# One step of a hybrid encoder layer: turning the running product of stick-breaking attention itself, with differences of v's rows, and loading the convolution's operands in pieces

## The chip, the cores and the metric

The kernel runs on one core of a Trainium2 chip. The metric is the device time of one execution in microseconds (us), the median over several runs. A TensorE is called PE below, a VectorE DVE, a ScalarE ACT, a GpSimd POOL and the engine that issues most transfers SP, as the profile names them.

## The reference

One layer over 1024 prompt frames and 32 sample frames (T = 1056 columns), D_MODEL 1024, 8 heads of 64:

```python
h = rmsnorm(x, g_mix)
q, k, v, cb, cc, cx, ga, gc = split(h @ w_in)
# stick breaking, strictly causal, per head
z = q @ k.T / sqrt(64);  mask = k_pos < q_pos
log_1m = where(mask, log_sigmoid(-z), 0)
tail = reverse_cumsum(log_1m) - log_1m          # keys after this one
a = where(mask, exp(log_sigmoid(z) + tail), 0)
y_attn = (a @ v) @ w_attn_out
y_conv = (cb * causal_conv3(cc * cx)) @ w_conv_out
x = x + (sigmoid(ga) * y_attn + sigmoid(gc) * y_conv) @ w_o
x = x + square(relu(rmsnorm(x, g_ffn) @ w_up)) @ w_down
x = x + sigmoid(rmsnorm(x, g_ple) @ w_ple_gate) * (p @ w_ple)
```

A last RMSNorm gives y; k, v and the last convolution rows are outputs too. In other words, with s = sigmoid(z), r = sigmoid(-z) = 1 - s and R[t,j] the product of r[t,i] over the keys i from j up to t-1, a weight is a[t,j] = s[t,j] R[t,j+1], which is also R[t,j+1] - R[t,j].

## The kernel before, in words

Everything is kept as channels by frames, and each float32 product on TensorE is three products of high and low parts (`wh`, `wl`; L642 to L644, L718 to L720, L932 to L934, L1616 to L1618), mostly with 128 rows, 128 columns of weights and 264 moving columns. By time the stages are:

- 0 to 332 us: the input projection `w_in`. Pairs of 512-column products are done with seven products of sums (the helper lines L213 to L215; results are put together on DVE in L249, L254, L259). What has to follow such a product (scaling by the norm, splitting, storing; `follow`, `values`, `conv_in`, `conv_gate`) is a generator in a list `side`, of which one piece is run after each product; `after(wait, gen)` lets `wait` pieces pass first. `conv_gate` (L554 to L562) forms the convolution's product with cb, splits it into high and low (`cvh` L558, L561) and stores it to `cvd`. `values` turns v (L509), splits it and stores it to `vd`. Tiles of 528 KB come from one pool (`blk`): a new tile takes a place whose last use, a transfer's reading included, has to be over.
- 332 to 629 us: attention. 64 steps (p, j, i): head pair p, head j, block i of 128 queries, which meets its i+1 blocks of 128 keys. The loop at the end of the stage goes through ORDER = "LSAFBFG": L weighs the step before (`weigh`: DVE scan L781 and product L782) and empties `pending`; S makes the scores (PE L759, L760; two sigmoids on ACT, L765; two causal fills on POOL, L773); A and B turn the step before that (`flip`: PE transposes of `s` L813, ACT cast to high L816, DVE low part L817); G gathers a finished pair of query blocks (`gather`: PE L834, ACT copy L843, DVE addition in `pending`); F fills with other TensorE work, a share given out by `spare(n)` and `shares()`: gate units, `last_gates`, `embed_unit` (L718 to L721) and `conv_unit` (weights cast L921, gate scaled on DVE L922, split L923, sigmoid on ACT L924, products L932). This part is scheduled in the written order. `conv_parts` (L857), called by the first embed unit, loads the eight 528 KB operands of the convolution from `cvd`. `branches_ahead`, after the last step, fetches and prepares the first weights of the next stage.
- 629 to 815 us: the two branch projections and `w_o`. Then the MLP: up with seven products, whose sums of the first set are made by `mid_sums(0, ...)` at once (L1396 to L1403) and of the others in `side`; mean squares of the norm (`mean_squares`, L1371); down to about 1465.
- 1465 to 1571: the gate of the embedding, in units u = 0 to 23. `post_c(u)` squares a finished unit on ACT (L1709) and adds it up on POOL (L1710). After the last unit comes `finish(23)`: sigmoid (L1764), loading of ACT's table with the root (L1765), product and residual on DVE (L1766, L1767), square (L1747), row sums on PE in two groups (`ps_early`, `ps_last`, L1740) added on DVE (L1749), root on ACT (L1750), reciprocal, three diagonals, a broadcast by PE (L1756), and the outputs.

Of the kernel before, what the change touches and what calls it, by code (L numbers as in the profile page):

```python
# [15 lines left out]
P = 128  # L16
# [33 lines left out]
def tile_step(  # L50
# [29 lines left out]
    keep = cpool.tile([P, 2, DEC], F32, name="keep")  # L80
    drop = cpool.tile([P, 2, DEC], F32, name="drop")
    for m_, a_, b_ in ((keep, 1.0, 0.0), (drop, 0.0, 1.0)):
        nc.gpsimd.memset(m_, a_)
        for p_ in range(4):
            r_ = m_[32 * p_ : 32 * p_ + 32, :, :]
            nc.gpsimd.affine_select(
                r_, r_, pattern=[[0, 2], [-1, DEC]], compare_op=ALU.is_gt, fill=b_, base=0, channel_multiplier=1
            )
# [357 lines left out]
    for p_ in range(4):  # L446
        nc.gpsimd.memset(vsT[p_], 0.0)

# [52 lines left out]
    def values(p, m):  # L501
# [3 lines left out]
        tm = blk(f"vt{p}", F32, [P, 8, P])  # L505
        for q0 in (0, 4):
            pt = tps.tile([P, 4, P], F32, tag="tp", name=f"pt_v{p}_{q0}")
            for i in range(4):
                nc.tensor.transpose(pt[:, i, :], m[:, (q0 + i) * P : (q0 + i + 1) * P], ident)  # L509
            nc.scalar.copy(tm[:, q0 : q0 + 4, :], pt)  # L510
            yield
        pt = tps.tile([P, 4, P], F32, tag="tp", name=f"pts_v{p}")
        nc.tensor.transpose(pt[:DEC, 0, :], m[:, SEQ:], ident)
        nc.scalar.copy(vsT[p][:DEC, :], pt[:DEC, 0, :])
        nc.sync.dma_start(v_out[p], tm)
        nc.sync.dma_start(v_sample[p], vsT[p][:DEC, :])
        for j in range(2):
            vs = blk(f"vs{p}{j}", F32R, [P, 8, P])
            src = tm[:, :, 64 * j : 64 * j + 64]
            nc.scalar.copy(vs[:, :, 0:64], src)  # L520
            dve(vs[:, :, 64:128], src, vs[:, :, 0:64].bitcast(F32), op=sub)
            nc.sync.dma_start(vd[p, j], vs.bitcast(F32).rearrange("p a c -> p (a c)"))
            yield
# [41 lines left out]
    def follow(nm, n, ms, wait=0):  # L565
# [11 lines left out]
        side.extend([after(wait, gens[0]), after(wait + (6 if nm in ("v", "cx") else 1), gens[1])])  # L577
# [87 lines left out]
    def last_gates(n):  # L665
# [38 lines left out]
    def embed_unit(n):  # L704
# [5 lines left out]
        def body(w):  # L710
            if n == 0:
                conv_parts()
# [36 lines left out]
    def scores(p, j, i):  # L749
# [12 lines left out]
        s = blk(f"s{p}{j}{i}", F32, [P, SEQ])  # L762
        r = apool.tile([P, SEQ], F32, tag="R", name=f"r{p}{j}{i}", bufs=3)
        for o, sign in ((r, -1.0), (s, 1.0)):
            nc.scalar.activation(o[:, :L].rearrange("p (h w) -> p h w", h=nh), zv, AF.Sigmoid, scale=sign)  # L765
        earlier(r[:, L - P : L], 1.0)
        earlier(s[:, L - P : L], 0.0)
        live[p, j, i] = (s, r, L)
# [8 lines left out]
    def sticks(s, r, L):  # L777


        rev = r[:, L - 1 :: -1] if L == r.shape[-1] else r[:, :L][:, ::-1]  # L780
        nc.vector.tensor_tensor_scan(rev, rev, rev, 1.0, ALU.mult, ALU.bypass)  # L781
        nc.vector.tensor_tensor(s[:, : L - 1], s[:, : L - 1], r[:, 1:L], op=ALU.mult)  # L782

    def weigh(p, j, i):
        sticks(*live[p, j, i])
# [6 lines left out]
    def flip(p, j, i):  # L792
        nm = f"{p}{j}{i}"
        s, _, L = live.pop((p, j, i))
# [14 lines left out]
        for b0 in range(0, i + 1, 4):  # L809
            nb = min(4, i + 1 - b0)  # L810
            pt = turned([P, 4, P], f"pa{nm}{b0}")
            for b in range(nb):
                nc.tensor.transpose(pt[:, b, :], s[:, (b0 + b) * P : (b0 + b + 1) * P], ident)  # L813
# [13 lines left out]
    def gather(p, j, c):  # L827
# [17 lines left out]
        pending.append(partial(dve, out, av[0:64, :], lo, op=add))  # L845
# [7 lines left out]
    def conv_parts():  # L853
        for i in range(4):
            for j, to in enumerate((ch, cl)):
                r = blk(f"cv{i}{j}", F32R)
                nc.sync.dma_start(r.bitcast(F32), cvd[i, j])  # L857
                to.append(r)
# [101 lines left out]
    def branches_ahead():  # L960
        for b in SEQ_B[:2]:
            branch_fetch(b)
        branch_high(SEQ_B[0])
        branch_scale(SEQ_B[0])
        branch_low(SEQ_B[0])
        branch_sigmoid(SEQ_B[0])
# [110 lines left out]
    def samples():  # L1077
# [12 lines left out]
        dve(r[:, :, PAST:], r[:, :, PAST:], drop, op=ALU.max)  # L1090
        dve(s[:, :, PAST:], s[:, :, PAST:], keep, op=ALU.mult)
        for j in range(2):
            sticks(s[:, j, :], r[:, j, :], LK)
# [68 lines left out]
    with tc.manual_schedule(engines=MM):  # L1162
        queries(0, 0, 0)
        queries(0, 0, 1)
        for n in range(LAST + 3):
# [30 lines left out]
            for p, c in splits.get(n, ()):  # L1196
                split_high(p, c)
            if n == LAST + 1:
                for _ in work:
                    pass  # L1200
                branches_ahead()
# [162 lines left out]
    def mean_squares():  # L1364
# [3 lines left out]
        for c in ts:  # L1368
# [3 lines left out]
            yield  # L1372
        for i in range(0, T, 132):
# [32 lines left out]
    def up_plain():  # L1406
# [19 lines left out]
        for _ in mid_sums(0, *m):  # L1426
            pass
# [274 lines left out]
    def post_c(u):  # L1702
# [4 lines left out]
        else:  # L1707
            q = tile_g(f"pq{u}", t)
            nc.scalar.square(q, xx)  # L1709
            pool(ssq, ssq, q, op=add)  # L1710
# [25 lines left out]
    def rows_of(src, name):  # L1736

        ps = tps.tile([P, 512], F32, tag="tp", name=name)
        for i in range(3):
            nc.tensor.matmul(ps[:LB, i : i + 1], src[:, i * LB : (i + 1) * LB], ones[:, 0:1], start=True, stop=True)  # L1740
        return ps[:LB, 0:3]

    def last_rows():

        n = KD - 1
        q = tile_g("ql", 2)
        dve(q, x1[n][:, lr], x1[n][:, lr], op=ALU.mult)  # L1747
        rl = cpool.tile([P, 3], F32, name="rl")
        dve(rl[:LB, :], rows_of(q, "ps_last"), seen["re"][:LB, :], op=add)  # L1749
# [250 lines left out]
```

## Time and profile before

| | |
|---|---|
| median of 3 runs | 1586.33 us (1585.05 to 1588.02) |
| profiled execution | 1587.34 us |
| its span | 1585.6 us |
| mean granted TensorE clock in it | 0.989 |
| PE busy | 1539.3 us (97%) |
| DVE busy | 1088.4 us (69%) |
| ACT busy | 771.8 us (49%) |
| POOL busy | 363.4 us (23%) |
| bytes by the large queue | 267.05 MB |

The table shows one engine that is busy nearly throughout. The views of the trace that the prediction uses give, for a stretch of the span, each engine's busy time with its number of instructions, the clock granted to TensorE (1.00 is full, 0.50 half), and for each instruction what ended the idle time ahead of it.

### The profile page before, as it was taken

The page shows a single profiled execution, that of the slowest core. Times are in us where ns is not written, and L with a number is a line of the kernel's source. Part 1 is how long each engine was busy: PE and PEld are TensorE (multiplying, and loading weights), DVE is VectorE, ACT ScalarE, POOL GpSimd, SP SyncE. Part 2 cuts the span into 40 slices and gives each one's busy share as a digit, 9 for nine tenths or more (in the row PEclk, how much of TensorE's full clock was granted, in tenths as well). Part 3 has the DMA queues.
Part 4 walks back from the last instruction along what each step waited for, and adds up shares of the span by engine and source line. Part 5 has one row for each costly group of instructions (what it writes and reads, how often), then busy time and mean ns, then how long its engine had stood idle before and what let it go on. Part 6 is the DMA issues. An engine that isn't in the chain of part 4 may idle for free.

```text
span 1585.6 us, 29812 instructions
## 1 busy us (share of the span) xinstructions
PE 1539.3 (97%) x11880; PEld 1523.2 (96%) x11880; DVE 1088.4 (69%) x1452; ACT 771.8 (49%) x1393; POOL 363.4 (23%) x411
## 2 busy tenths in 40 slices
PE   8999999999999978999999999999999999999997
PEld 8999999999999968999998999999999999999996
DVE  7568465767887866674558555555567896799866
ACT  6644444355566655332355555555644334444544
POOL 2223332012322211101311222222020131013353
PEclk9999999999999989999999999999999999999998
DMA  6513355473343544344344444434786897683443
GB/s 230 191 54 131 147 201 192 93 233 113 108 123 106 207 141 147 133 169 162 142 165 156 149 143 148 140 141 149 264 307 195 270 333 248 199 271 110 127 137 109
DMA packets 110523, 268.98 MB, mean 170 GB/s; under 512 B 13072, under 2 KB 30096, under 8 KB 110384
## 3 DMA queue, kind: packets, MB, share of 16 engines
q1 hardware_dynamic: 110240, 267.05, 49.6%
q8 instruction: 93, 1.52, 0.4%
q14 instruction: 46, 0.38, 0.1%
q10 hardware_dynamic: 144, 0.03, 0.0%
HBM read 186.31 MB, written 80.72 MB: 168 GB/s over the span
## 4 chain that ended last, share of the span: by engine, by line
PE 85%; DVE 6%; DMA 3%; ACT 3%; issue 2%; POOL 1%; SPq 0%; DVEq 0%; ACTq 0%; POOLq 0%
PE ps_dn L1618 6%; PE ps_dn L1616 6%; PE ps_dn L1617 6%; PE ps_A11u L213 3%; PE ps_A11u L214 3%; PE ps_A11u L215 3%; PE ps_g L642 3%; PE ps_g L643 3%; PE ps_g L644 3%; PE ps_A11i L215 3%; PE ps_A11i L213 3%; PE ps_A11i L214 3%; PE av L834 2%; PE ps_wo L1305 2%; PE ps_wo L1307 2%; PE ps_wo L1306 2%
## 5 line engine op out<-in xcount | busy, mean ns | idle before, releaser
L1618 PE MATMUL ps_dn<-fh,wlo_dn 128*128 128x264 f32 x896 | 255.0, 285 | 2.4 <-DVE wlo_dn L1509 2.4
L1616 PE MATMUL ps_dn<-fh,whi_dn 128*128 128x264 f32 x896 | 254.7, 284 | 0.0
L1617 PE MATMUL ps_dn<-fl,whi_dn 128*128 128x264 f32 x896 | 254.6, 284 | 0.0
L1618 PEld LDWEIGHTS ps_dn<-fh,wlo_dn 128*128 128x128 f32 x896 | 168.7, 188 | 2.9 <-DVE wlo_dn L1509 2.8
L1616 PEld LDWEIGHTS ps_dn<-fh,whi_dn 128*128 128x128 f32 x896 | 168.6, 188 | 0.1
L1617 PEld LDWEIGHTS ps_dn<-fl,whi_dn 128*128 128x128 f32 x896 | 168.5, 188 | 0.0
L642 PE MATMUL ps_g<-B,whi_g 128*128 128x264 f32 x384 | 115.4, 300 | 0.0
L643 PE MATMUL ps_g<-B,whi_g 128*128 128x264 f32 x384 | 109.4, 285 | 0.0
L644 PE MATMUL ps_g<-B,wlo_g 128*128 128x264 f32 x384 | 109.1, 284 | 0.0
L1509 DVE TENSOR_TENSOR wlo_dn<-raw_dn,whi_dn 128x1024 fp32r<-128x1024 f32 x40 | 69.7, 1742 | 29.7 <-ACT whi_dn L1503 29.2
L773 POOL TENSOR_SCALAR_AFFINE_SELECT r<-r 128x128 f32<-128x128 f32 x64 | 32.9, 513 | 248.8 <-ACT r L765 238.4
L781 DVE TENSOR_TENSOR_SCAN r<-r 128x128 f32<-128x128 f32 (+3 forms) x64 | 86.7, 1355 | 0.2 <-POOL r L773 0.2
L200 POOL TENSOR_TENSOR s_u<-raw_u,raw_u 128x512 f32<-128x512 f32 x30 | 44.2, 1473 | 185.1 <-DVE slS_u L163 173.4
L1561 POOL TENSOR_TENSOR c<-c,rs 128x528 f32<-128x528 f32 x16 | 26.7, 1668 | 244.8 <-DVE c L1625 122.8
L1503 ACT CAST whi_dn<-raw_dn 128x1024 fp32r<-128x1024 f32 x40 | 42.1, 1051 | 78.7 <-PE ps_dn L1617 78.7
L200 POOL TENSOR_TENSOR s_i<-raw_i,raw_i 128x512 f32<-128x512 f32 x24 | 32.7, 1362 | 187.6 <-DVE slS_i L163 169.3
L817 DVE TENSOR_TENSOR at<-pa,at 128x512 fp32r<-128x512 f32 (+2 forms) x96 | 51.9, 553 | 34.6 <-ACT at L816 31.0
L642 PEld LDWEIGHTS ps_g<-B,whi_g 128*128 128x128 f32 x384 | 72.4, 189 | 0.6 <-issue 0.5
L643 PEld LDWEIGHTS ps_g<-B,whi_g 128*128 128x128 f32 x384 | 72.4, 189 | 0.0
L644 PEld LDWEIGHTS ps_g<-B,wlo_g 128*128 128x128 f32 x384 | 72.3, 188 | 0.0
L214 PE MATMUL ps_A11u<-T,shS_u 128*128 128x264 f32 x240 | 68.3, 285 | 1.7 <-DVE T L157 1.7
L1529 DVE TENSOR_TENSOR fl<-mr,fh 128x1056 fp32r<-128x1056 f32 x56 | 69.9, 1248 | 0.0
(431 smaller groups left out, 5575.3 us busy)
## 6 DMA issues: line engine op xcount, KB each, us to landing
raw_dn<-in_w_down_dram SPq DMA_DIRECT2D x56, 512.0 KB, 4.5
mr<-mdT SPq DMA_DIRECT2D x32, 528.0 KB, 5.6
raw_u<-in_w_up_dram SPq DMA_DIRECT2D x32, 512.0 KB, 3.6
raw_i<-in_w_in_dram SPq DMA_DIRECT2D x28, 512.0 KB, 4.4
mdB<-m SPq DMA_DIRECT2D x48, 264.0 KB, 2.4
mr<-mdB SPq DMA_DIRECT2D x24, 528.0 KB, 6.1
raw_pg<-in_w_ple_gate_dram SPq DMA_DIRECT2D x17, 512.0 KB, 3.5
gd<-sg SPq DMA_DIRECT2D x16, 528.0 KB, 3.4
```

Source lines behind the costliest of these rows:

```text
L200: f()
L213: nc.tensor.matmul(p_, wh[:, k, :], o[:, 0, c], start=new and n == 0, stop=False, **on)
L214: nc.tensor.matmul(p_, wh[:, k, :], o[:, 1, c], start=False, stop=False, **on)
L215: nc.tensor.matmul(p_, wl[:, k, :], o[:, 0, c], start=False, stop=z, **on)
L642: nc.tensor.matmul(ps, wh[:, k, :], o[:, 0, q], start=i == 0, stop=False)
L643: nc.tensor.matmul(ps, wh[:, k, :], o[:, 1, q], start=False, stop=False)
L644: nc.tensor.matmul(ps, wl[:, k, :], o[:, 0, q], start=False, stop=i == 7)
L781: nc.vector.tensor_tensor_scan(rev, rev, rev, 1.0, ALU.mult, ALU.bypass)
L1529: dve(l, mraw.pop(v), opd[v].bitcast(F32), op=sub)
L1616: nc.tensor.matmul(ps, hi[:, j, :], oh, start=j == 0, stop=False)
L1617: nc.tensor.matmul(ps, hi[:, j, :], ol, start=False, stop=False)
L1618: nc.tensor.matmul(ps, lo[:, j, :], oh, start=False, stop=j == NP_ - 1)
```

## The change

1. Attention: the sum over keys is made by parts. With R as above, the output is the sum over j of R[t,j] (v[j-1] - v[j]) plus the last row of v that the pair of query blocks has. So the second sigmoid, the second causal fill and the product L782 go; the scanned `r` itself is turned (its tile has 4 places, not 3); the block of the later keys, which the earlier query block doesn't have, is filled with 1 in the high part; the addition after the gather also adds `vlast`. The constants in `spare` are smaller. `sticks` stays for the sample frames, which are worked per head j now.
2. `values`: v is stored as it is (its turning is left to the host's view of the output), a copy `dv` holds the differences of neighbouring rows, and `dv` is turned and split straight from PSUM.
3. The second generator of `cb` waits four pieces, not one.
4. `conv_parts` becomes `conv_part(i)`: two loads with each of four pieces of the last gates.
5. `branches_ahead` is spread over steps LAST-5 to LAST+1; `mid_sums` of the first set goes to `side`, three pieces late; `mean_squares` gives way once more after each sum.
6. The end: the last-but-one unit's square is added on DVE inside `finish`, behind the loading of the table; the row sums are gathered in one PSUM group, and the root reads PSUM directly; one of three diagonals is made on ACT.

```diff
 def values (the part that follows scaling)
-        tm = blk(f"vt{p}", F32, [P, 8, P])
...
+        nc.sync.dma_start(v_out[p], m[:, :SEQ])
+        dv = blk(f"dv{p}", F32, [P, SEQ])
+        nc.scalar.mul(dv[:, 0:1], m[:, 0:1], -1.0)
+        dve(dv[:, 1:], m[:, : SEQ - 1], m[:, 1:SEQ], op=sub)
+        for j in range(2):
+            nc.scalar.copy(vlast[:, p, j, :], m[64 * j : 64 * j + 64, 255:SEQ:256])
+        yield
...
-            nc.scalar.copy(vs[:, :, 0:64], src)
-            dve(vs[:, :, 64:128], src, vs[:, :, 0:64].bitcast(F32), op=sub)
...
+                h, src = vs[j][:, q0 : q0 + 4, 0:64], pt[:, :, 64 * j : 64 * j + 64]
+                nc.scalar.copy(h, src)
+                dve(vs[j][:, q0 : q0 + 4, 64:128], src, h.bitcast(F32), op=sub)
...
-        side.extend([after(wait, gens[0]), after(wait + (6 if nm in ("v", "cx") else 1), gens[1])])
+        side.extend([after(wait, gens[0]), after(wait + {"v": 6, "cx": 6, "cb": 4}.get(nm, 1), gens[1])])
...
                         if c:
                             p_split(2 * i + t - 2)
+                            conv_part(2 * i + t - 2)
...
-            if n == 0:
-                conv_parts()
...
-        for o, sign in ((r, -1.0), (s, 1.0)):
-            nc.scalar.activation(o[:, :L].rearrange("p (h w) -> p h w", h=nh), zv, AF.Sigmoid, scale=sign)
+        nc.scalar.activation(r[:, :L].rearrange("p (h w) -> p h w", h=nh), zv, AF.Sigmoid, scale=-1.0)
         earlier(r[:, L - P : L], 1.0)
-        earlier(s[:, L - P : L], 0.0)
...
     def weigh(p, j, i):
-        sticks(*live[p, j, i])
+        remains(*live[p, j, i])
...
-                nc.tensor.transpose(pt[:, b, :], s[:, (b0 + b) * P : (b0 + b + 1) * P], ident)
+                nc.tensor.transpose(pt[:, b, :], r[:, (b0 + b) * P : (b0 + b + 1) * P], ident)
...
-                nc.gpsimd.memset(A[hl][b // 4][:, b % 4, 0:P].bitcast(F32), 0.0)
+                nc.gpsimd.memset(A[hl][b // 4][:, b % 4, 0:P].bitcast(F32), 1.0 - hl)
...
-        pending.append(partial(dve, out, av[0:64, :], lo, op=add))
+        end = vlast[:, p, j, c : c + 1]
+        pending.append(partial(nc.vector.scalar_tensor_tensor, out, av[0:64, :], end, lo, op0=add, op1=add))
...
-    def conv_parts():
-        for i in range(4):
-            for j, to in enumerate((ch, cl)):
-                r = blk(f"cv{i}{j}", F32R)
-                nc.sync.dma_start(r.bitcast(F32), cvd[i, j])
-                to.append(r)
+    def conv_part(i):
+        for j, to in enumerate((ch, cl)):
+            r = blk(f"cv{i}{j}", F32R)
+            nc.sync.dma_start(r.bitcast(F32), cvd[i, j])
+            to.append(r)
...
-        u = 0.435 * scan + 0.2 * (scan > 0) + 0.17 * turn + 0.12 * (turn > 0)
+        u = 0.28 * scan + 0.13 * (scan > 0) + 0.17 * turn + 0.12 * (turn > 0)
...
-        for _ in mid_sums(0, *m):
-            pass
+        side.append(after(3, mid_sums(0, *m)))
...
 def finish(u)
         nc.scalar.activation(g_, g_, AF.Sigmoid)
         nc.scalar.preload_act_table_set("sqrt_and_others")
+        post_c(u - 1, dve)
         dve(g_, ems.pop(u)[:, lr], g_, op=ALU.mult)
         dve(xx, xx, g_, op=add)
-        seen["re"] = cpool.tile([P, 3], F32, name="re")
-        nc.scalar.copy(seen["re"][:LB, :], rows_of(seen["ssq3"][:, lr], "ps_early"))
-        pr = last_rows()
+        q = tile_g("ql", 2)
+        dve(q, xx, xx, op=ALU.mult)
+        ps = tps.tile([P, 512], F32, tag="tp", name="ps_last")
+        rows_into(ps, seen["ssq3"][:, lr], True)
+        rows_into(ps, q, False)
+        pr = last_rows(ps)
```

SP's queue of transfers near the end of attention (`cv` are the convolution's operands, `raw_pw`, `raw_oc` raw weights, `q311` the queries of a step, `ed` takes finished embedding rows `em`). Before:

```order
L857 DMA cv21_7170<-cvd_167 128x1056
L857 DMA cv30_7172<-cvd_167 128x1056
L857 DMA cv31_7174<-cvd_167 128x1056
L99 DMA raw_pw3_7247<-in_w_ple_dram 128x256
L745 DMA q311_7271<-qd_164 64x2x256
L746 DMA q311_7271<-qd_164 64x256
L747 DMA q311_7271<-qd_164 64x256
L723 DMA ed_168<-em0_7176 128x1056
```

The same place in the changed kernel:

```order
L862 DMA cv30_6985<-cvd_167 128x1056
L862 DMA cv31_6987<-cvd_167 128x1056
L690 DMA gd_143<-sg15_6388 128x1056
L99 DMA raw_pw2_6990<-in_w_ple_dram 128x256
L99 DMA raw_pw3_7059<-in_w_ple_dram 128x256
L750 DMA q311_7091<-qd_164 64x2x256
L751 DMA q311_7091<-qd_164 64x256
L728 DMA ed_168<-em0_6992 128x1056
```

Before, all eight `cv` loads stand together ahead of these rows; now `cv00` to `cv11` stand some 14 rows earlier, `cv20` and `cv21` seven rows earlier, and only the last pair stands here, ahead of the last gate's store.

ACT's queue around the first convolution unit (`cw0` is its weights' high part, `sc0` its gate), with what each row waits for. Before:

```order
L816 CAST at30400_7291<-pa3040_7295 128x4x128 [waits PE_49,Pool_49]
L721 COPY em1_7249<-ps_pw1528_7302 128x264 [waits PE_49]
L816 CAST at30401_7293<-pa3044_7310 128x128 [waits PE_49]
L721 COPY em1_7249<-ps_pw1792_7316 128x264 [waits PE_49]
L921 CAST cw0_7325<-raw_oc0_7147 128x512 [waits DMAHW7_49,DMAHW1_49,Activation_49]
L924 ACTIVATE sc0_7149<-sc0_7149 128x1056 [waits DVE_49]
```

The same place in the changed kernel:

```order
L821 CAST at30400_7107<-pa3040_7111 128x4x128 [waits PE_49]
L726 COPY em1_7061<-ps_pw1792_7118 128x264 [waits PE_49]
L821 CAST at30401_7109<-pa3044_7127 128x128 [waits PE_49]
L926 CAST cw0_7133<-raw_oc0_6975 128x512
L929 ACTIVATE sc0_6977<-sc0_6977 128x1056 [waits DVE_49]
```

The cast of `cw0` waits for two transfers before and for none now; the sigmoid of the gate waits for DVE in both.

DVE's queue in the input projection, where one product's `cb` rows are split (`cvh`) and the next product's results are put together (`m1_i5`, `m2_i5`). Before:

```order
L561 TENSOR_TENSOR m1_i4_1313<-m1_i4_1313,cvh0_1672 128x1056
L249 TENSOR_TENSOR m1_i5_1576<-ps_A12i5_0_1701,p1_i50_1578 128x264 [waits DVE_49,PE_49]
L561 TENSOR_TENSOR m2_i4_1314<-m2_i4_1314,cvh1_1694 128x1056 [waits Activation_49]
L249 TENSOR_TENSOR m1_i5_1576<-ps_A12i5_1_1717,p1_i51_1579 128x264 [waits PE_49]
L254 TENSOR_TENSOR m2_i5_1577<-ps_A11i5_0_1584,s5_i50_1582 128x264 [waits DMAHW4_49,DMAHW3_49,DMAHW6_49,DVE_49,PE_49]
```

The same place in the changed kernel:

```order
L567 TENSOR_TENSOR m1_i4_1314<-m1_i4_1314,cvh0_1671 128x1056 [waits DVE_49]
L560 TENSOR_TENSOR m2_i4_1315<-m2_i4_1315,yc1_1490 128x1056 [waits DVE_49]
L249 TENSOR_TENSOR m1_i5_1577<-ps_A12i5_0_1699,p1_i50_1579 128x264 [waits PE_49]
L249 TENSOR_TENSOR m1_i5_1577<-ps_A12i5_1_1713,p1_i51_1580 128x264 [waits PE_49]
L254 TENSOR_TENSOR m2_i5_1578<-ps_A11i5_0_1585,s5_i50_1583 128x264 [waits DVE_49,PE_49]
```

The first writing of `m2_i5` waits for three transfer queues before and for none now; the second split (`cvh1`) has moved behind it.

More of the change, by code (lines that the diff above doesn't have):

```diff
@@ L504, in values @@
             yield
-        tm = blk(f"vt{p}", F32, [P, 8, P])
+        nc.sync.dma_start(v_out[p], m[:, :SEQ])
[5 more added lines that the diff above has]
+        yield
+        pt = tps.tile([P, 4, P], F32, tag="tp", name=f"pts_v{p}")
+        nc.tensor.transpose(pt[:DEC, 0, :], m[:, SEQ:], ident)
+        nc.scalar.copy(vsT[p][:DEC, :], pt[:DEC, 0, :])
+        nc.sync.dma_start(v_sample[p], vsT[p][:DEC, :])
+        yield
+        vs = [blk(f"vs{p}{j}", F32R, [P, 8, P]) for j in range(2)]
         for q0 in (0, 4):
@@ L1734, in everywhere, with rows_into, last_rows @@
         nc.scalar.copy(dst[:, q0 * P : q0 * P + w], pr[:, :w])
[L1736 to L1738 removed]
+    def rows_into(ps, src, first):
         for i in range(3):
[L1740 to L1747, printed above, removed]
+            nc.tensor.matmul(
+                ps[:LB, i : i + 1], src[:, i * LB : (i + 1) * LB], ones[:, 0:1], start=first and i == 0, stop=not first and i == 2,
+                skip_group_check=True,
+            )
+    def last_rows(ps):
         rl = cpool.tile([P, 3], F32, name="rl")
[L1749 to L1750 removed]
+        nc.scalar.activation(rl[:LB, :], ps[:LB, 0:3], AF.Sqrt, bias=eps_t[:LB], scale=1.0 / D)
         nc.vector.reciprocal(rl[:LB, :], rl[:LB, :])
```

74 lines of the change are left out of this document (37 added, 37 removed).

## Prediction

> **What bounds the kernel now.** I read the page's first part, then PE's list of waits, then a table of windows, and only then single instructions. The page:
>
> ```profile
> PE 1539.3 (97%) x11880; PEld 1523.2 (96%) x11880; DVE 1088.4 (69%) x1452; ACT 771.8 (49%) x1393; POOL 363.4 (23%) x411
> ```
>
> Only PE is near its span, so an edit pays where PE stands idle or runs at a lower clock, and nowhere else. PE's waits (engine, line, who ended it: total, times, longest):
>
> ```profile
> PE ps_oc L932 <- ACT cw L921: 6.8, 1, 6.8
> ...
> PE ps_pw L718 <- ACT em L721: 5.7, 7, 2.2
> PE ps_A11i L213 <- DVE m_i L254: 2.4, 2, 2.2
> PE ps_oc L117 <- DVE oT L1204: 2.4, 1, 2.4
> ...
> PE ps_A11u L214 <- DVE T L157: 1.7, 1, 1.7
> PE ps_ms L1370 <- DVE rs L1371: 1.5, 1, 1.5
> ```
>
> They are few and long. The windows say where they lie and what follows them (columns: length, busy time and count for PE, PEld, DVE, ACT, POOL, granted clock, DMA share, GB/s):
>
> ```profile
> 139.00:146.00 7.00, 4.78 (x26) 4.57 (x26) 4.13 (x9) 0.90 (x2) 2.27 (x2) 0.76 0.95 387
> 146.00:332.00 186.00, 186.00 (x1528) 185.75 (x1526) 113.67 (x148) 79.60 (x166) 40.71 (x27) 1.00 0.49 165
> 333.00:543.00 210.00, 208.90 (x1699) 203.93 (x1699) 167.10 (x222) 128.17 (x278) 56.18 (x158) 1.00 0.41 127
> 543.00:629.00 86.00, 69.34 (x445) 63.16 (x443) 59.72 (x89) 50.66 (x115) 14.09 (x38) 0.88 0.46 167
> 556.00:563.50 7.50, 0.67 (x6) 0.41 (x4) 0.07 (x1) 0.72 (x2) 0.00 (x0) 0.69 0.96 344
> 563.50:572.50 9.00, 8.26 (x32) 7.28 (x33) 8.79 (x10) 5.63 (x12) 1.60 (x2) 0.50 0.21 62
> 572.50:589.00 16.50, 15.58 (x116) 14.72 (x116) 10.41 (x23) 10.02 (x28) 3.40 (x12) 1.00 0.25 90
> 591.60:600.00 8.40, 7.72 (x36) 7.34 (x37) 6.32 (x10) 4.61 (x11) 1.69 (x5) 0.59 0.37 124
> ```
>
> ```profile
> 826.00:840.00 14.00, 12.35 (x101) 12.14 (x100) 12.21 (x16) 9.65 (x20) 5.89 (x4) 1.00 0.72 243
> ```
>
> Two things are to be seen. Attention up to 543 us is already bound by PE: 1.1 of 210 us idle. Its end is not: in the 86 us from 543 to 629 PE makes 445 matmuls, which at the pace of the undisturbed 572.5 to 589 (16.5 / 116 = 0.142 us each) are 63.3 us. So about 22.7 us are lost there, and an idle time is followed by matmuls at half clock: 32 in 9.0 us at clock 0.50, 36 in 8.4 us at 0.59.
>
> **The conv loads.** The 6.8-us wait is followed back through the chain of waits, the SP queue and ACT (start, duration, what; in brackets the idle time ahead):
>
> ```profile
> 548.13 10.22 DMA cv<-cvd
> ...
> 558.41 4.36 DMA ed<-em
> ```
>
> ```profile
> 543.98 5.61 SPq L857 DMA_DIRECT2D cv<-cvd  x8
> ```
>
> ```profile
> 562.78 0.62 ACT L921 CAST cw<-raw_oc 128x512 fp32r<-128x512 f32 x1 [9.06 <-DMA ed<-em]
> ```
>
> Eight loads are issued together and occupy the queues until 558.4; the store of `em` stands behind them, and `cw0` takes a place that this store has to free. Price: 6.8 us idle, and at half clock 9.0 us for 32 matmuls that at 0.142 us are 4.5, so 4.5 lost; together 11.3. In the change three of the four pairs stand before the other transfers of this place, the fourth is 2 of 8 loads (10.22 / 4 = 2.6 us), and the cast waits for no transfer. I take **-11.0**; if a quarter of the old stall is left, -9.
>
> **The second stall.** At 589.3 PE waits 2.2 us for an `em` copy behind ACT's sigmoid of the gate:
>
> ```profile
> 588.50 1.24 DVE L922 TENSOR_TENSOR sc<-sc,rs 128x1056 f32<-128x1056 f32 x1
> ...
> 589.78 1.08 ACT L924 ACTIVATE sc<-sc 128x1056 f32<-128x1056 f32 x1 [1.15 <-DVE sc L922]
> ```
>
> The window 591.6 to 600 has 36 matmuls, 5.1 us at 0.142, in 8.4: 3.3 lost. With the wait 5.5. The edit takes one product (L782) and one sigmoid per step from the two engines:
>
> ```profile
> L781 DVE TENSOR_TENSOR_SCAN r<-r 128x128 f32<-128x128 f32 (+3 forms) x64 | 86.7, 1355 | 0.2 <-POOL r L773 0.2
> L782 DVE TENSOR_TENSOR s<-s,r 128x127 f32<-128x127 f32 (+3 forms) x64 | 49.3, 771 | 7.6 <-POOL s L773 0.9 <-POOL r L773 0.5
> L813 PE MATMUL pa<-ident,s 128*128 128x128 f32 x288 | 48.0, 276 | 0.5 <-DVE s L782 0.5
> L765 ACT ACTIVATE s<-z 128x128 f32<-128x128 f32 (+3 forms) x64 | 41.4, 646 | 0.0
> ```
>
> L782 at some 0.77 us stands in DVE's queue shortly ahead of L922, so the 1.15-us wait of ACT falls to about 0.4 and PE's 2.2 to about 0.8 to 1.4. The 1.7-us wait for `T`, in the window 826 to 840, brought no low clock (1.00), this one did: I take 0.8 left and no half clock, 5.5 - 0.8 = **-4.7**. The other `em` waits (5.7 - 2.2 = 3.5 us in six) stand behind the same ACT queue, which loses 0.65 us a step: **-2.0**.
>
> [...]
>
> **The end of attention.** 2.4 us, for this row of DVE:
>
> ```profile
> 626.34 1.25 DVE L886 TENSOR_TENSOR sa<-sa,rs 128x1056 f32<-128x1056 f32 x1
> ...
> 628.49 0.42 DVE L1204 TENSOR_TENSOR oT<-av,avl 64x256 f32<-64x256 f32 x1
> ```
>
> `branches_ahead` now scales three steps sooner, so 1.25 us go from in front of L1204; a split of `oT` on the way to the last row stays: **-1.1**. The four prices, 11.3 + 5.5 + 3.5 + 2.4, are the 22.7 us that the windows gave, so no other large loss hides there; of them I expect 11.0 + 4.7 + 2.0 + 1.1 = 18.8 back.
>
> **Attention before 543.** DVE and ACT lose 49.3 and 41.4 us by the rows above (POOL its second fill), PE none: 288 transposes stay, of r in place of s. At most the 1.1 us idle there can come: **-0.9**.
>
> **The input projection.** At 139 us:
>
> ```profile
> 141.21 0.43 DVE L254 TENSOR_TENSOR m_i<-ps_A11i,s_i 128x264 f32<-128x264 f32 x1 [1.62 <-DMA cvd<-cvh]
> ```
>
> ```profile
> 135.89 0.86 SPq L559 DMA_DIRECT2D cvd<-cvh  x2
> ```
>
> `m2_i5` takes the place of `cvh`, whose store was issued 5 us earlier. With `cb` three pieces later it gets another place, and the row waits for no transfer. The window has 26 matmuls in 7.0 us; at 186 / 1528 = 0.122 us they are 3.2: **-3.8**. In `values` the work grows. Before, per head pair, two differences of 1.08 us; after, one of about 1.2 (1023 wide, by L922's 1.24 for 1056) and four of 256 columns a partition (0.42 each, the row of that width): +0.7 us, four times 2.9:
>
> ```profile
> L521 DVE TENSOR_TENSOR vs<-vt,vs 128x512 fp32r<-128x512 f32 x8 | 8.6, 1075 | 0.8 <-ACT vs L520 0.8
> ```
>
> ```profile
> L817 DVE TENSOR_TENSOR at<-pa,at 128x256 fp32r<-128x256 f32 x16 | 6.7, 418 | 2.7 <-ACT at L816 2.5
> ```
>
> From 146 to 332 DVE is busy 113.67 of 186 us and PE throughout, so the cover is 72 us: **0**. If the chain of a `values` piece met a PE that waits for PSUM, it would cost one such operation, 1.2 us; it may as well spare one copy (0.6).
>
> **The MLP.** `mid_sums` made at once stands ahead of `T` and of `rs`:
>
> ```profile
> 829.79 1.80 DVE L1396 TENSOR_TENSOR ta<-m 128x528 f32<-128x528 f32 x1
> ...
> 833.18 0.71 DVE L1403 TENSOR_TENSOR tb<-m,ta 128x528 f32<-128x528 f32 x1
> ```
>
> Spread over later products, four operations of 0.7 to 1.8 us are no longer queued ahead of one wait, and `rs` gets a piece more of time: 1.7 + 1.5 = **-3.2**.
>
> **The tail.** Here a wait is added. Before:
>
> ```profile
> 1571.76 0.44 ACT L1709 ACTIVATE pq<-xx 128x288 f32<-128x288 f32 x1 [2.06 <-POOL xx L1700]
> 1572.11 0.43 ACT L1764 ACTIVATE pgsl<-pgsl 128x288 f32<-128x288 f32 x1
> 1572.55 1.28 ACT L1765 ACT_TABLE_LOAD   x1
> 1572.57 1.09 DVE L1766 TENSOR_TENSOR pgsl<-em,pgsl 128x288 f32<-128x288 f32 x1 [0.57 <-ACT pgsl L1764]
> ...
> 1574.26 0.46 DVE L1747 TENSOR_TENSOR ql<-xx 128x288 f32<-128x288 f32 x1
> ...
> 1575.76 0.30 ACT L1750 ACTIVATE rl<-rl,eps_t 96x3 f32<-96x3 f32 x1 [1.49 <-DVE rl L1749]
> ```
>
> After, ACT's order is sigmoid (1572.0), table (to 1573.7), square (to 1574.1); DVE's sum of squares waits for that, and the product of L1766, which needs only the sigmoid, is queued behind the sum. Four DVE operations of 0.46 then end at 1575.95, where the square ended at 1574.72 before: +1.2. The root then reads PSUM directly, with no addition between, and one of three diagonals goes to ACT beside DVE's two, for which I take a third off: **+0.8**, between 0 and +1.5. [...]
>
> **The sum.** -18.8 - 0.9 - 3.8 + 0 - 3.2 + 0.8 = -25.9. The profiled span 1585.6 becomes 1559.7, its execution (1587.34, 1.7 us more than its span) 1561.4; that execution lay 1.0 above the median of 1586.33, so **1560.4 us**. If nothing were left of the 22.7, the tail cost nothing and `values` spared its copy: 3.9 + 0.8 + 0.6 less, 1555. If a quarter of the conv stall (2.5 more), 1.4 us of the second (0.6 more) and 1.2 us of `values` are left: 1564.7.
>
> **The rivals.**
>
> *The second stall stays* (ACT waits in order for DVE, and PE's idle time again ends in half clock). For it: DVE's 59.7 us, less the products, lie in a stage of 67 us instead of 86. Against it: L782 is gone from just ahead of it. Then -4.7 is 0: 1565.1; if it happens at two conv units, 1569.8. Chance 0.15.
>
> *The loads don't spread enough*: the fourth pair and the queries behind it fill the queues as before, so that a wait moves from `cw0` to the queries. For it: DMA share 0.96 in 556 to 563.5; bytes are the same. Against: 0.41 from 333 to 543, with room for three pairs. A stall of 3 us (a pair's 2.6 and its hand-over) with a half clock of 3.3 then remains: 1566.7. Chance 0.10.
>
> *Slower*: the steps become a chain. With less filler given to long steps (`spare` falls from 0.435 to 0.28 a block), the transposes of r wait for the scan in each step; from (25.9 + 3.2) / 64 = 0.45 us a step on, the kernel is slower by 0.2% or more; at 0.6 us it takes 1560.4 + 38.4 = 1599. For it: the scan is 1.36 us on average and is now read at once. Against: PE waited for L782 once, 0.5 us, in 64 steps (row of L813), and L782 itself came after the scan. Chance 0.04.
>
> *No change*: the reliefs are taken back by new waits of the same size. Chance 0.03.
>
> **How the numbers follow.** Forecast 0.68, rivals 0.32. The range takes the forecast's own 1555 to 1564.7, with 2 us below for smaller waits in stages that I left at nothing, and reaches over the first two rivals: 1553 to 1568. A difference of 0.2% (3.2 us) is about what a measurement of this kernel can tell from none: faster 0.92, within it 0.03, slower 0.05.
>
> **What would show it.** PE's waits without `cw` L921 over 2 us and without `m_i` by a DMA; clock 1.00 in all windows up to 1571; the stage 543 to 629 some 19 us shorter; the same 1699 matmuls of attention in about 209 us; ACT's square behind the table in the tail, with `ql` about 1.2 us later after the last `ps_pg`. I am wrong if a window at 0.5 to 0.8 stays in attention, or PE waits for the scan in many steps.

## The result, and the profile after

The changed kernel takes 1573.09 us (median of 4, 1571.12 to 1574.38), the kernel before beside it 1586.48 us (4 runs, 1585.05 to 1588.02). The ratio is 0.9914, with a 95% interval of 0.9897 to 0.9931: 13.4 us faster, half of the 26 us that were forecast, and above the range of 1553 to 1568. One execution of a version told below, of 1582.58 us by its median, took 3857.68 us; it is not in that version's ratio, and its trace is not used.

PE's list of waits in the profiled execution after (span 1572.7 us) answers the one of before:

```profile
PE ps_pw L723 <- ACT em L726: 6.3, 6, 2.6
...
PE ps_last L1748 <- DVE ssq L1719: 3.6, 1, 3.6
...
PE ps_oc L117 <- DVE oT L1213: 1.9, 1, 1.9
PE ps_oc L939 <- DVE cw L928: 1.4, 1, 1.4
...
PE ps_oc L937 <- ACT cw L926: 1.0, 1, 1.0
...
PE ps_A11i L213 <- DVE m_i L254: 0.6, 2, 0.4
```

The 6.8-us wait for `cw`, the wait at 139 us for `m_i` and the waits for `T` and `rs` of the MLP are gone. The waits for `em` are not: 6.3 us against 5.7, and the longest is 2.6. The windows after (columns as in the prediction) give the stages:

```profile
139.00:146.00 7.00, 6.58 (x54) 6.36 (x54) 5.66 (x10) 4.30 (x8) 1.99 (x2) 1.00 0.66 263
329.00:543.00 214.00, 213.24 (x1733) 208.38 (x1732) 139.09 (x182) 106.77 (x235) 30.90 (x107) 1.00 0.46 147
543.00:616.00 73.00, 61.55 (x417) 56.38 (x416) 47.61 (x70) 40.65 (x95) 9.47 (x24) 0.95 0.39 138
...
554.96:558.38 3.42, 3.42 (x14) 2.93 (x14) 2.14 (x3) 1.10 (x4) 0.00 (x0) 0.50 0.14 38
582.27:585.69 3.42, 3.42 (x16) 3.42 (x14) 0.99 (x2) 1.74 (x4) 0.58 (x3) 0.50 0.95 334
616.40:619.82 3.42, 3.42 (x14) 3.42 (x13) 0.80 (x2) 0.00 (x0) 2.43 (x1) 0.50 1.04 408
```

Attention up to 543 us has 0.8 us of idle time left (1.1 before). Its end, 543 to 616, holds 417 matmuls in 73 us; at the 0.142 us of the undisturbed stretch that is 59.2, so 13.8 us are still lost where 3.9 were forecast. Ahead of the tail there are three stretches of half clock, 3.41 us each, where before there were three, of 3.4 us from 142.5, 13.7 from 558.9 and 6.8 from 593.0. Attention can be measured in each trace from the first score to the first branch product. Before and after, the rows of these two tiles (duration least, median and most in ns, then first and last start):

```profile
L759 PE MATMUL z<-ks,q x96: 220/340/522, 332.5 to 608.9; 128*128 128x384 f32 x24, 128*128 128x512 f32 x24, 128*128 128x320 f32 x16, 128*128 128x448 f32 x16
L117 PE MATMUL ps_oc<-cv,whi_oc x72: 320/323/427, 629.0 to 692.3; 128*128 128x352 f32 x72
```

```profile
L764 PE MATMUL z<-ks,q x96: 219/341/628, 329.9 to 597.3; 128*128 128x384 f32 x24, 128*128 128x512 f32 x24, 128*128 128x320 f32 x16, 128*128 128x448 f32 x16
L117 PE MATMUL ps_oc<-cv,whi_oc x72: 320/323/498, 615.9 to 680.7; 128*128 128x352 f32 x72
```

From 332.5 to 629.0 are 296.5 us, from 329.9 to 615.9 are 286.0: attention is 10.5 us shorter, the input projection 2.6. The MLP from its first product into `ps_A11u` to its first of down gives 2.9 more (311.9 to 309.0 us), the branches lose 1.3 (a half-clock stretch lies in their start), down and the gate lose 0.2, the tail loses 1.5: together the 13.0 us by which the span is shorter.

What holds the end of attention now is seen first in ACT's waits and in the chain of waits there:

```profile
ACT whi_pw L108 <- DMA raw_pw<-in_w_ple_dram: 4.1, 1, 4.1
...
ACT sc L929 <- DVE sc L927: 2.5, 2, 1.4
```

```profile
540.47 8.33 DMA raw_pw<-in_w_ple_dram
548.88 0.41 ACT whi_pw L108
```

A 128 KB weight takes 8.3 us from issue to landing; the median of the weight loads of that line from 520 to 600 us is 2.5. SP's list says what was issued ahead of it:

```profile
536.61 0.99 SPq L874 DMA_DIRECT2D sc<-gd  x2
537.70 0.88 SPq L862 DMA_DIRECT2D cv<-cvd  x2
540.06 0.32 SPq L690 DMA_DIRECT2D gd<-sg  x1
540.47 1.48 SPq L99 DMA_DIRECT2D raw_pw<-in_w_ple_dram  x2
```

Five transfers of 528 KB in 3.8 us, the last pair of `cv` among them. DMA share is 0.8 or more from 520 to 549 us.

### The profile page after: what moved, and what is told of

Same layout as the page of the kernel before. It is cut to its first block, busy times and chain, and to the rows that moved or that the text cites. A ratio compares the mean times of both kernels' runs of the same rounds, so it can differ in the third digit from the quotient of the medians.

```text
span 1572.7 us, 29473 instructions
## 1 busy us (share of the span) xinstructions
PE 1535.2 (98%) x11880; PEld 1520.4 (97%) x11880; DVE 1050.9 (67%) x1401; ACT 737.3 (47%) x1341; POOL 332.3 (21%) x346
## 4 chain that ended last, share of the span: by engine, by line
PE 88%; DVE 5%; DMA 2%; ACT 2%; issue 1%; POOL 1%; SPq 0%; DVEq 0%; ACTq 0%; POOLq 0%
PE ps_dn L1627 6%; PE ps_dn L1625 6%; PE ps_dn L1626 6%; PE ps_A11u L213 4%; PE ps_A11u L214 4%; PE ps_A11u L215 4%; PE ps_g L648 3%; PE ps_g L649 3%; PE ps_g L650 3%; PE ps_A11i L215 3%; PE ps_A11i L213 3%; PE ps_A11i L214 3%; PE av L839 2%; PE ps_wo L1316 2%; PE ps_wo L1315 2%; PE ps_wo L1314 2%
## 5 line engine op out<-in xcount | busy, mean ns | idle before, releaser
L775 POOL TENSOR_SCALAR_AFFINE_SELECT r<-r 128x128 f32<-128x128 f32 x64 | 28.3, 442 | 283.0 <-ACT r L768 275.7
L782 DVE TENSOR_TENSOR_SCAN r<-r 128x128 f32<-128x128 f32 (+3 forms) x64 | 87.7, 1371 | 0.1
```

## Experiments

All times are medians; the kernel before ran beside each, at 1584.4 to 1587.3 us. Where the changed kernel is the base, its 1573.1 us is meant.

**The loads alone, in the kernel before.** `conv_parts` becomes `conv_part` as in the change, and:

```diff
                             p_split(2 * i + t - 2)
+                            conv_part(2 * i + t - 2)
...
-            if n == 0:
-                conv_parts()
```

> The kernel before with the convolution loads in four pairs and nothing else of the change. Theory of the queues (the loads fill the transfer queues wherever they stand, and what is fetched just behind them comes late): the 6.8-us wait at cw goes, but a wait of 2 to 4 us for a late embedding weight or query comes in its place, so about half of the 11.3 us comes back: 1579 to 1583. Rival, the prediction's step (three pairs are hidden in attention, nothing is late): the whole 11 us, 1575 to 1576.

1579.26 us, ratio 0.996 (0.9946 to 0.9975). The wait for `cw` of 6.8 us is gone, and attention is 7.3 us shorter (332.0 to 621.2). This fits the theory of the queues in size, but not in mechanism: no engine waits for a late weight or query. PE's waits of 2.1 (`em`), 1.7 (`cw`'s low part) and 1.5 us (`sc`) stay, and the transfers that are waited for behind them are stores that have to free a place: the low part of `at` takes that of `sg15` (DVE waits 2.4 us), an `em` that of `em0` (ACT waits 1.7 us). That the number came out was luck. The wait for `cw` went with its place here, too: `cw0` takes the one that the tile `s304` of attention had, and its cast waits for no transfer.

**Parts 3, 4 and 5 without the rewritten attention.** The edits are those of the diff for `cb`, `conv_part`, `branches_ahead`, `mid_sums` and `mean_squares`.

> The kernel before with parts 3, 4 and 5 of the change (cb's second half later, loads in pairs, branches_ahead, mid_sums and mean_squares spread), without the rewritten attention, values and tail. Theory that attention is bound by PE and its end by order and transfers: the rewrite is worth 2 to 4 us and the new tail costs 1.5, so 1573 to 1576. Rival, that the relief of DVE and ACT carries the gain: 1580 or more.

1580.31 us, ratio 0.9964 (0.9952 to 0.9975): no better than the loads alone. My theory expected 1573 to 1576 and missed. A wait of 2.7 us stands at the start of attention, where the kernel before has 0.6 and the changed one none. PE's list, and ACT's rows around it, in this kernel:

```profile
PE z L758 <- ACT s L764: 2.7, 1, 2.7
```

```profile
329.56 0.28 ACT L764 ACTIVATE r<-z 128x128 f32<-128x128 f32 x1
331.65 1.07 ACT L558 CAST cvh<-m_i 128x1056 fp32r<-128x1056 f32 x1 [1.81 <-DVE m_i L554]
332.63 0.27 ACT L764 ACTIVATE s<-z 128x128 f32<-128x128 f32 x1
```

`cb`'s cast, three pieces later now, stands between the two sigmoids of the first step, waits for DVE there, and the scores' one PSUM buffer is not free until the second sigmoid has read it. 330 to 338.5 us show a clock of 0.60. In the changed kernel, with a single sigmoid, PE does not wait there.

**The same with `cb` early again.**

> The kernel of the third to fifth part without attention, and cb's second half early again. Theory that the later cb piece puts its cast between the two sigmoids of the first step and so costs 2.7 us of waiting and 3 us of low clock at 330 us, which the single sigmoid of the changed kernel doesn't meet: this wait goes, the one at 139 us (3.3 to 3.8) returns, 1580.3 - 5.8 + 3.5 = 1578. Rival, that the wait at 330 us has another cause: it stays and the time is 1583 or more.

1579.41 us, ratio 0.9952 (0.9939 to 0.9966). The wait at 330 us goes and the one for `m_i` returns (2.1 us), as the theory said; the mean clock of the profiled execution is 0.995, where it was 0.990 with `cb` late; the gain is 1 us where 2 were expected, within what the runs spread.

**The changed kernel with `cb` early.**

```diff
-{"v": 6, "cx": 6, "cb": 4}.get(nm, 1)
+{"v": 6, "cx": 6}.get(nm, 1)
```

> The changed kernel with cb's second half again one piece late. Theory: the wait for the store of cvh at about 139 us returns with its half clock, 3.3 to 3.8 us more than the changed kernel's 1573.1: 1576.4 to 1576.9, PE waiting 2 us for m_i. Rival, that the rest of the change had moved the store away anyway: 1573.

1576.22 us, ratio to before 0.9937 (0.9922 to 0.9952): 3.1 more. The first score comes at 333.1 us, not 329.9, and PE waits 2.3 us for `m_i` again.

**Six of eight loads left out.**

```diff
         for j, to in enumerate((ch, cl)):
+            if i:
+                to.append(to[0])
+                continue
```

> The changed kernel with six of the eight convolution loads left out (all four blocks use the first block's operands, so the convolution branch is computed from other data). Theory of the queues: raw_pw lands in time, the waits of 2.5, 1.0 and 1.4 us at 547 to 554 us and the low clock behind them go, 5 to 6 us less: 1567 to 1568. Rival, that ACT's and DVE's order there makes the stall: 1572 or more, with ACT waiting for DVE in place of the transfer.

1567.85 us, 5.2 less; ACT doesn't wait for `raw_pw`, and the waits of 2.5 and 1.0 us are gone.

**The third embedding weight ahead of the loads.**

```diff
-        return lambda: (gate_fetch_(n), gate_fetch_(n + 1)), prepare, body, (24, 2), 28
+        return lambda: (gate_fetch_(n), gate_fetch_(n + 1)), prepare, body, (24, 3), 28
...
             if n == after - 8:
-                for i in range(CFILL):
-                    branch_fetch(("c", i))
-            elif n >= after:
+                branch_fetch(("c", 0))
+            if n == after + 8:
+                branch_fetch(("c", 1))
+            if n >= after:
```

> The changed kernel with the third embedding weight fetched with the first two, ahead of the convolution loads, and the second convolution unit's weight and gate fetched later (a raw buffer and 0.8 MB less in the jam). Theory of the queues: ACT no longer waits 4.1 us for raw_pw, PE's 2.5-us wait at 547 us goes, 4 to 6 us less: 1567 to 1569. Rival, that the next transfer is late in its place: within 2 us of 1573.

1567.99 us, 5.1 less, with all eight loads: the same gain as leaving six of them out. So the eight loads need not cost these 5 us. The edit also fetches the second convolution unit's weight and gate later; how much of the 5 us that gives is not separated.

**The gate's sigmoid out of ACT's way.**

```diff
-            nc.scalar.activation(sg, sg, AF.Sigmoid)
...
+                    if k == 1:
+                        nc.scalar.activation(mg[n][:, c], mg[n][:, c], AF.Sigmoid)
```

> The changed kernel with the gate's sigmoid of the two convolution units taken out of the preparation and made in three parts just ahead of its use. Theory that PE's 2.6-us wait at 578 us is ACT waiting in order for DVE's scaling: ACT's 1.1-us wait goes, with it 2 us of idle time and perhaps the low clock behind (1.6): 2 to 4 us less, 1569 to 1571. Rival, that DVE is simply behind there: PE still waits over 2 us, 1572 to 1573.

1569.95 us, 3.1 less. PE's 2.6-us wait is gone, and ACT's list from 555 to 620 us has no wait for the scaling any more; the mean clock is 0.994, where it was 0.993. In the changed kernel the rows were these (ACT, DVE, PE):

```profile
579.12 1.08 ACT L929 ACTIVATE sc<-sc 128x1056 f32<-128x1056 f32 x1 [1.14 <-DVE sc L927]
580.11 0.39 ACT L108 CAST whi_pw<-raw_pw 128x256 fp32r<-128x256 f32 x1
```

```profile
577.50 0.42 DVE L822 TENSOR_TENSOR at<-pa,at 128x256 fp32r<-128x256 f32 x1 [0.38 <-ACT at L821]
577.84 1.25 DVE L927 TENSOR_TENSOR sc<-sc,rs 128x1056 f32<-128x1056 f32 x1
```

```profile
580.83 0.39 PE L723 MATMUL ps_pw<-ph,whi_pw 128*128 128x264 f32 x1 [2.59 <-ACT em L726]
```

ACT's wait for the scaling is 1.14 us, as it was 1.15 before the change. DVE was idle for 0.38 us just ahead, waiting for ACT's cast of `at`: it was not behind. The chain is that cast, DVE's low part of `at`, the scaling of 1.25 us, the sigmoid; ACT has only the cast of `cw` to do meanwhile, and the weight that PE needs next is queued behind the sigmoid. The kernel before, where DVE had no idle time just ahead, had the same chain:

```profile
587.74 0.38 ACT L816 CAST at<-pa 128x256 fp32r<-128x256 f32 x1
```

```profile
588.17 0.41 DVE L817 TENSOR_TENSOR at<-pa,at 128x256 fp32r<-128x256 f32 x1
```

DVE begins at 588.17 what ACT has made ready at 588.12, so it could not have begun sooner.

**The square ahead of the table load.**

```diff
         dve(g_, pgs.pop(u), seen["rs3"][:, lr], op=ALU.mult)
+        post_c(u - 1, dve)
         nc.scalar.activation(g_, g_, AF.Sigmoid)
         nc.scalar.preload_act_table_set("sqrt_and_others")
-        post_c(u - 1, dve)
```

> The changed kernel with the last-but-one square again ahead of the sigmoid and the table load, still added on DVE. Theory that the square behind the table load holds DVE's chain: 1.7 us less from the last gate product to the end, 1571 to 1571.5. Rival, that POOL's addition in the residual is what the chain waits for: under 0.5 us less.

1569.41 us, 3.7 less. From the last gate product to the end the traces show 16.0 us in the changed kernel (1556.7 to 1572.7) and 13.0 in this one (1554.3 to 1567.3): 3.0 less, 1.9 of it PE's wait for `ssq`, which falls from 3.6 to 1.6. More than the 1.7 expected; in this execution the matmuls behind it were also shorter (the broadcast took 0.88 us, not 1.57, the row sums of `ql` 0.67, not 1.05; in the changed kernel these stand at a clock of 0.50 to 0.58), which is the other 1.1.

**The first attention branch behind the last gather.**

```diff
...
+        branch_high(SEQ_B[1])
         split_high(3, slice(768, T))
         split_low.pop()()
+        branch_scale(SEQ_B[1])
+        branch_sigmoid(SEQ_B[1])
+        branch_low(SEQ_B[1])
```

> The changed kernel with the first attention branch's weight cast, scaling and sigmoid written behind the last gather. Theory that the 1.9-us wait at 614 us is the last copy standing behind that sigmoid on ACT: it falls to about 1 us, and the low clock behind it (1.6 us) may go: 0.9 to 2.5 us less, 1570.5 to 1572.2. Rival, that the moved work delays the first branch products instead: 1573 or more.

1572.68 us, which the runs cannot tell from 1573.1. The trace shows the shorter wait that was expected: PE's last wait is 1.0 us, not 1.9; but in the same execution the first wait (`raw_pw`) was 3.3 us long, not 2.5, and the mean clock is 0.993, as in the changed kernel. Alone it is inconclusive by time.

**All four, and a fifth.** The fifth puts the low part of the convolution's weights ahead of the scaling:

```diff
             nc.scalar.copy(w[:, 0], raw)
-            dve(sg, sg, rs, op=ALU.mult)
             dve(w[:, 1], raw, w[:, 0].bitcast(F32), op=sub)
+            dve(sg, sg, rs, op=ALU.mult)
```

> The changed kernel with the four edits that were tried singly: early third embedding weight, late gate sigmoid, square ahead of the table, first attention branch behind the last gather. Theory, that they are separate stalls: 5.1 + 3.1 + 3.0 (by the trace of the tail) + 1 less than 1573.1, 1560 to 1562. Rival, that one relief moves the next wait forward: 1564 or more.

> As the kernel with the four edits, and in the convolution units the weights' low part ahead of the gate's scaling on DVE. Theory that PE's 1.1-us wait for the low part at the first unit is this order: about 1 us less than that kernel, 1559 to 1561. Rival, that the gate's scaling is then late: the same or more.

With four 1561.61 us, ratio 0.9836 (0.9823 to 0.985); with five 1560.48 us, ratio 0.9828 (0.9815 to 0.9842), faster than both kernels. The sum of the single gains, 12.3 us with four, came to 11.5. The windows of the version with five edits show the end of attention without half clock (418 matmuls in 62.7 us, 59.4 at 0.142):

```profile
543.00:605.70 62.70, 58.47 (x418) 53.59 (x416) 46.03 (x68) 40.05 (x98) 8.57 (x24) 1.00 0.47 162
```

**Attention and `values` alone.** The kernel before with parts 1 and 2 and nothing else.

> The kernel before with parts 1 and 2 alone (turned running product, values, sample frames by head, spare), all else as before. Theory that attention is bound by PE and the stalls at its end by order and transfers: only the small waits get shorter, 1 to 4 us less than before, 1582 to 1585. Rival, that the relief of DVE and ACT carries the change: 1579 or less.

1573.66 us, ratio 0.9916 (0.9900 to 0.9933): as fast as the whole change. Here my theory fell, and the prediction's with it, since the eight loads are still issued together and yet `cw` costs PE 0.5 us, not 6.8. PE's list and the whole execution:

```profile
PE ps_pw L724 <- ACT em L727: 5.4, 4, 2.6
...
PE ps_A11i L213 <- DVE m_i L254: 2.4, 2, 2.2
...
PE ps_oc L117 <- DVE oT L1211: 1.9, 1, 1.9
```

```profile
139.00:146.00 7.00, 4.83 (x40) 4.62 (x39) 4.46 (x9) 1.28 (x3) 2.16 (x2) 1.00 0.97 393
...
11.00:1560.00 1549.00, 1524.83 (x11859) 1510.86 (x11857) 1039.15 (x1378) 730.50 (x1329) 328.77 (x325) 1.00 0.50 171
```

ACT's queue says why. The row of `cw0` in this kernel, and below it the one of the kernel with held places (told further down):

```
L928 CAST cw0_7133<-raw_oc0_6963 128x512
L934 CAST cw0_7321<-raw_oc0_7144 128x512 [waits DMAHW7_49,Activation_49]
```

The cast waits for no transfer here. The tiles `s`, three or so at a time, are no longer taken from the pool, and `cw0` gets a place that is long free (a tile `B22` of the gates had it, as in the changed kernel), and not the one of `em0`, whose store stands behind the loads. That the clock is 1.00 from 11 to 1560 us of this execution is luck in part, as the last section shows.

**The loads together again, in the changed kernel.**

> The changed kernel with the eight convolution loads issued together by the first embed unit again, all else as changed. Theory of the places (the wait at cw went with the tiles s, not with the spreading; the spreading only makes raw_pw late): no wait at cw, raw_pw in time, the losses of 543 to 630 us fall from 18 to about 12, 1567 to 1568.5. Rival, the prediction's step: the 6.8-us wait and its low clock return, 11 us more, 1584.

1570.81 us, ratio 0.9899 (0.9882 to 0.9915), 2.3 less than the changed kernel: no wait for `cw` over 0.5 us returns. Undoing the spreading doesn't cost 11 us; by the medians it gains 2, though the two ratios' intervals overlap. The 5 us that I expected are not reached, since another weight is then 2.0 us late and PE still waits 6.1 us for `em`, at a mean clock of 0.994 where the changed kernel has 0.993.

**The old loads in the fast version.**

> The changed kernel with the loads together again and the edits at the gate's sigmoid, the weights' low part, the square and the first attention branch, without the early third embedding weight. Theory: the loads together make one transfer of an embedding weight 1.6 us late, as in parts 1 and 2 alone, so 1 to 3 us slower than the fastest so far (1560.5): 1561.5 to 1563.5. Rival, that the spreading costs in itself: 1559 or less.

1565.83 us, 5 more than with the loads spread and the weight early; a weight is 3.0 us late and PE waits 3.7. I expected 1 to 3. The loads together with the early weight were not run, so what the place of the loads costs by itself stays open.

**Places held by tiles that nothing uses.** First with a tile `s` per step that is given back at once:

> Parts 1 and 2 alone, but each step again takes a place of the pool for a tile s of which only one column is written (by POOL) and which nothing reads. ACT, DVE and PE have the relief, the places are as before. Theory of the places: cw's cast again waits for a transfer to free its place, 5 us or more of PE's time with the low clock behind come back: 1579 to 1585. Rival, that the relief of ACT and DVE removed the wait: 1573 to 1575.

1570.64 us, ratio 0.9906 (0.9888 to 0.9923), and no wait for `cw`. The test missed its aim: `cw0` then got the place of `sg15`, whose store was long done. So the tile was kept as long as `s` had been:

```diff
+        s = blk(f"s{p}{j}{i}", F32, [P, SEQ])
+        nc.gpsimd.memset(s[:, 0:1], 0.0)
...
+            nc.gpsimd.memset(s[:, 1:2], 0.0)
```

> Parts 1 and 2 alone, and each step keeps a place of the pool for an unused tile s as long as the kernel before did (POOL writes one column of it at the scores, and another when the step is turned). ACT, DVE and PE have the whole relief, but cw's cast waits for the store of em0 as before. Theory of the places: PE waits 4 to 7 us for cw and then runs at half clock for 3 to 4 us, 1573.7 + 7 to 11 = 1580 to 1585. Rival, that the relief of ACT and DVE removed the wait: 1571 to 1575.

1582.58 us, ratio 0.9981 (0.9971 to 0.9991): 9 us are lost again, with all the relief of ACT and DVE in place. The trace is of another execution of the same kernel:

> The same kernel once more, for its trace. Theory of the places: PE waits 4 to 7 us for ACT's cast of cw, and that cast for the transfer ed, which is queued behind the eight loads; 1580 to 1585 us. Rival: no such wait, and the 9 us more than without the held places are spread over many small ones.

1583.33 us in one run. PE's list, ACT's row and the chain of waits:

```profile
PE ps_oc L945 <- ACT cw L934: 11.9, 1, 11.9
```

```profile
562.73 0.62 ACT L934 CAST cw<-raw_oc 128x512 fp32r<-128x512 f32 x1 [11.35 <-DMA ed<-em]
```

```profile
545.51 10.02 DMA cv<-cvd
...
555.60 7.05 DMA ed<-em
```

The wait of the kernel before is back, with `cw0` in the place of `em0` again, and longer; ACT comes to this cast sooner, and the store lands as late (562.65 us, where it was 562.77). This settles it: the wait was for a place in the pool, and either edit, the spreading or the rewrite, gave `cw0` another place.

## Why the prediction was wrong, point by point

**The conv loads (-11.0).** This is the step that failed. It said that the wait goes because the loads are spread. The wait went, but in the attention rewrite alone it goes too (1573.66 us), and it comes back when the places are held (1582.58). Attention lasts 281.1 us with the rewrite alone (331.0 to 612.1) and 291.5 with the places held (333.0 to 624.5): of the 15.4 us by which the rewrite alone shortens it, 10.4 go with the place and 5.0 with the relief. These are two single executions, the first at a clock of 1.00 from 543 to 612 us, the second at 0.92 from 543 to 624.5; by the medians the place is worth 8.9 us. The diff named the place (the tile `s` leaves the pool), and I priced it as engine time only. The other half of the step, that nothing is late behind the spread loads (a rest of 0.3 us of the 11.3), is what cost the time.

**What took its place.** Five large transfers were issued within 4 us, and the next embedding weight came 8.3 us after its issue. With that weight fetched early the kernel is 5.1 us faster, so its lateness costs some 5 us; with the loads together again it is 2.3 us faster, with intervals that overlap, so how much of the 5 us the spreading itself brought stays open. That was my second rival (a wait on what stands behind the last pair), with 1566.7 and a chance of 0.10; it came at a weight, not at the queries. Of 2.5 + 1.0 + 1.4 us of waits and 3.41 - 14 x 0.142 = 1.4 of half clock, 6.3 in all, the early weight gave 5.1 back. Of the 13 us that are missing, this is about 6, the second stall 3, the end of attention with the half clock behind it 2; the rest is spread over the small terms.

**The second stall (-4.7).** Failed as well: my first rival came true. I took ACT's wait for a DVE that is behind; it is an order, ACT standing in line for a 1.25-us operation that DVE has only just been given. L782 stood in the queue (587.02 to 587.58), but not on this chain: DVE's L817 could not begin before ACT's cast ended at 588.12. The wait changed from 1.15 to 1.14 us. The half clock behind it was shorter (3.41 us from 582.27, where before there were 6.83 from 593.03), which is all that this term gave, and may be luck. Moving the sigmoid gave 3.1 us.

**The small `em` waits (-2.0).** Without the two long ones 6.3 - 2.5 - 2.6 = 1.2 us are left of 3.5, where 1.5 were forecast: right.

**The end of attention (-1.1).** 2.4 to 1.9 us, and a half-clock stretch behind it that was not there before (1.4 us, in the branches): no gain. ACT's sigmoid of the first attention branch now stands ahead of the last copy.

**Attention before 543 (-0.9), the input projection (-3.8), `values` (0), the MLP (-3.2).** Attention before 543 gave 0.3 of its 0.9: 0.8 us of idle time are left in 214 us, where it was 1.1 in 210. The others are right in mechanism and near in size: undoing `cb` costs 3.1; the input projection gave 2.6, which leaves some 0.5 for `values`, within what the runs spread; the MLP gave 2.9.

**The tail (+0.8).** The mechanism was right, the size was 1.5; 0.4 of the difference is that the row sums of `ql` took 1.05 us at a clock of 0.58 (1561.7 to 1562.9), where before they took 0.64 at 1.00. Rows after:

```profile
1557.62 0.44 ACT L1773 ACTIVATE pgsl<-pgsl 128x288 f32<-128x288 f32 x1 [2.40 <-DVE pgsl L1772]
1558.08 1.28 ACT L1774 ACT_TABLE_LOAD   x1
1559.38 0.44 ACT L1718 ACTIVATE pq<-xx 128x288 f32<-128x288 f32 x1
1559.92 0.46 DVE L1719 TENSOR_TENSOR ssq<-ssq,pq 128x288 f32<-128x288 f32 x1 [2.39 <-ACT pq L1718]
...
1562.87 0.26 ACT L1756 ACTIVATE rl<-ps_last,eps_t 96x3 f32<-96x3 f32 x1 [3.05 <-PE ps_last L1748]
```

The square begins 0.02 us after the table load ends, and the load 0.02 us after the sigmoid ends; the load takes 1.28 us, as it did before.

**The slower rival.** Nothing of it: PE waits for the scan in no step.

**Two edits that lean on each other.** Parts 3 to 5 without the rewrite gave 6 us, the rewrite alone 13, both 13 (with the new tail, which costs 1.5 of them). The loads' spreading and the rewrite remove the same wait, so they don't add; and the later `cb` costs a wait at 330 us unless the second sigmoid is gone.

## What to carry to other kernels

A wait for a transfer at the first writing of a tile can be a wait for its place, as here: ask whose place it is, and how many tiles the edit adds to or takes from that pool, before counting engine time. Spreading large loads over a stage can leave a small transfer that the next step needs behind them, as it did here (8.3 us to landing). In the queue of an engine, look for the instruction that waits a whole operation of another engine, and move what is needed sooner ahead of it; where several stalls are priced, try which single edits remove the same one, since those gains don't add.

## What the runs showed of the hardware that I had not expected

The length of the idle time alone does not tell whether half clock follows. After 1.9 us of idle time at 614 us the changed kernel runs 3.41 us at 0.50 (616.40 to 619.82); with the rewrite alone PE idles 2.2 us at 139, 2.3 at 556 and 2.6 us at 576, and the clock is 1.00 from 139 to 146 and from 543 to 612 us.

One kernel differs in it from execution to execution, too: the four executions of the kernel with the rewrite alone have mean clocks of 0.997, 0.995, 0.992 and 0.997 and took 1572.05, 1575.28, 1577.47 and 1572.04 us. What decides it, these traces leave open.
